# Placing the TensorE operands of a fp32r decoder step at chosen start addresses

## The chip, the cores and the metric

The kernel runs on one core of one Trainium2 chip. The metric is the device time of one execution in microseconds (us), the median of several runs. All engine times below come from one profiled execution of the kernel.

## The reference

One inference step of one decoder layer, for 256 new prompt tokens and 8 decode tokens together, with model width 2048. The large products are a first SwiGLU feed-forward (2048 to 5632 and back), an input projection to a mixer (RWKV-7 heads beside a convolution), an output projection, a memory cross-attention with its key, value, query and output projections, and a second SwiGLU:

```python
def trunk_layer(x, shift_prev, conv_prev, wkv_prev, mk, mv, p):
    x = layer_norm(ALPHA * x + 0.5 * swiglu(x, p['ffn1_w1'], p['ffn1_w3'], p['ffn1_w2']), ...)
    mix, sh, cv, wkv = parallel_mixer(x, shift_prev, conv_prev, wkv_prev, p)
    x = layer_norm(ALPHA * x + mix, ...)
    x = layer_norm(ALPHA * x + mem_attend(x, mk, mv, p['w_mq'], p['w_mo']), ...)
    x = layer_norm(ALPHA * x + 0.5 * swiglu(x, p['ffn2_w1'], p['ffn2_w3'], p['ffn2_w2']), ...)
    return x, sh, cv, wkv
```

Every weight is fp32 and is read once from HBM; the result must be close to fp32.

## The kernel before

Activations lie transposed, features on the 128 partitions and the T = 264 tokens along the free axis, so 2048 features are 16 tiles of 128 x 264. To reach fp32 accuracy with fp32r matmuls, every operand is split into a high part (rounded to fp32r) and a low part (the rest), and each product is three matmuls into the same accumulator (`mm3`, L301 to L305): high weights by high activations, high weights by low activations, low weights by high activations. In each of them the weights, 128 x 128, are the stationary operand, loaded anew for every matmul, and a 264-column activation tile is the moving operand.

Weights arrive in 512 KB chunks (128 x 1024) by SyncE's queue into `wraw` (3 buffers), ScalarE rounds each into `whi` (L188), and VectorE subtracts that from the raw chunk into `wlo` (L189); `whi` and `wlo` have 4 buffers each. The order of all the chunks is a plan written beforehand; side work (norms, RWKV heads, convolution, decode attention) is woven in as generators that step when the planned time of the main stream reaches them. `gemm` (L318) runs over the chunks; a chunk 256 columns wide uses each activation tile for two weight slices in a row, one 128 wide (the last two of each feed-forward's output, and some of the mixer's) for one.

The high and low activation tiles live in these pools:

- `act`: `xh0`, `xl0` to `xh15`, `xl15`, and the residual tiles `y0` to `y15`; in the second feed-forward the first 16 gate pairs reuse the `x` places.
- `ffn1` and `ffn2`: gate pairs `gh`, `gl`.
- `raw`: `rh`, `rl`, 266 columns each, the input of the second feed-forward, and the memory tokens in the attention stage.
- `mem`: `mh`, `ml`, 256 columns, the memory tokens during the first norm. In `mem_kv` the keys take the memory tile as moving operand; the values swap the roles, so there `whi` and `wlo` are the moving operands and the memory tiles the weights.

A tile of 264 fp32 columns takes 1,056 bytes of each partition, which is 4 x 256 + 32. Pools lie one behind another in SBUF in the order in which they are opened, and a tile's size is rounded up to 32 bytes, so the place of each tile follows from the sizes ahead of it. `place` (L82) allocates a pool's tiles in a stated order with gaps in bytes between them, which fixes their places for the rest of the pool's life. The constants' pool begins at byte 16,512 and holds 7,168 bytes, so `wraw` begins at 23,680, and `whi`, `wlo` and `act` (68,736) all at a multiple of 256 plus 128. As the buffers are 4,096 bytes and a slice of 128 columns 512, every weight slice begins at 128 modulo 256. The gap of 224 ahead of `act` puts the first `xh` at 96 modulo 256, and the tiles follow at steps of 32: `xh` and `xl` of an even tile at 96 and 128, of an odd one at 160 and 192, then a filler (four `y` tiles or 128 bytes) that brings the next even tile to 96 again. `gate_places` does the same. `rh` and `rl` begin at 96 and 160, `mh` and `ml` at 128.

Of the kernel before, what the change touches and what calls it, by code (L numbers as in the profile page):

```python
# [8 lines left out]
F32 = mybir.dt.float32  # L9
F32R = mybir.dt.float32r  # L10
# [8 lines left out]
KD = 16  # L19
TP = 256  # L20
TB = 8
T = TP + TB
DFF = 5632
# [17 lines left out]
class Side:  # L41


    def __init__(self, tc, gen, at, pace=1.0):
        self.tc, self.gen, self.next, self.done, self.pace = tc, gen, at, False, pace
# [8 lines left out]
class Builder:  # L54
    def __init__(self, tc, I, O, es):
        self.tc, self.nc, self.I, self.O = tc, tc.nc, I, O
        self.n = 0
        P = lambda name, bufs, **kw: es.enter_context(tc.tile_pool(name=name, bufs=bufs, **kw))
        self.const = P("const", 1)
        self.wraw = P("wraw", NRAW)  # L60
        self.whi = P("whi", NSPLIT)
        self.wlo = P("wlo", NSPLIT)
        self.act = P("act", 1)
        self.places()
        self.tmp = P("tmp", 2)
        self.acc = P("acc", 4, space=PSUM)
        self.mis_stack = es.enter_context(ExitStack())
        self.banks()
        self.dram = P("dram", 1, space=DRAM)
        self.t = 0.0  # L70
        self.sides = []
        self.plan, self.raws, self.split = [], [], []
        self.nraw = self.nsplit = self.nused = self.nres = 0
# [15 lines left out]
                tag, cols, dt = t  # L89
                pool.tile([128, cols], dt, tag=tag, name=self.uid(tag))  # L90

    def places(self):


        order = [224]
        for q in range(KD // 2):
            for k in (2 * q, 2 * q + 1):
                order += [(f"xh{k}", T, F32R), (f"xl{k}", T, F32R)]
            order += [(f"y{m}", T, F32) for m in range(4 * q, 4 * q + 4)] if q < KD // 4 else [128]
        self.place(self.act, *order)  # L100

    def gate_places(self, pool, first, gap):
        order = [gap]
        for i in range(first, DFF // 256, 2):
            for k in (i, i + 1):
                order += [(f"gh{k}", T, F32R), (f"gl{k}", T, F32R)]
            order.append(128)
        self.place(pool, *order)

    def uid(self, s):  # L110
        self.n += 1
        return f"{s}_{self.n}"

    def ct(self, shape, name, dt=F32):
        return self.const.tile(shape, dt, tag=name, name=name)

    def misc(self):
# [1255 lines left out]
    def att_start(self, pool):  # L1373
        nc = self.nc
        self.mx = pool
        self.banks(1)
        self.mem_reload()
        eye = self.mt("eye", (128, TB, TB), F32R)
        z = self.mt("eye0", (128, TB * TB))
        nc.vector.memset(z, 0.0)  # L1380
        nc.vector.memset(z[:, 0 : TB * TB : TB + 1], 1.0)
        nc.scalar.activation(eye.rearrange("p a b -> p (a b)"), z, AF.Copy)
        self.eye = eye
        self.kvn = {}
        self.qs = {}
        self.oh = None
# [304 lines left out]

PRETURN = 5
RAW, RENORM = 2, 0.6
GAPS = 128, 224, 96, 128
TS = 384
LASTCOLS = [(1536, 256), (1792, 128), (1920, 128)]
CONV_GAP = 2.5
# [25 lines left out]
def program(tc, I, O):  # L1723
    with ExitStack() as es:
# [10 lines left out]
        with tc.tile_pool(name="mem", bufs=1) as mpool:  # L1735
            b.place(mpool, GAPS[0])
            with tc.tile_pool(name="ffn1", bufs=1) as pool:
                b.gate_places(pool, 0, GAPS[1])
                b.xs = b.load_x(mpool)
# [31 lines left out]
        def after():  # L1771
            mix.close()
            b.raw = es.enter_context(tc.tile_pool(name="raw", bufs=1))
            for k in range(KD):
                b.place(b.raw, 128 if k else GAPS[2], (f"rh{k}", T + 2, F32R), (f"rl{k}", T + 2, F32R))
            b.att_start(att.enter_context(tc.tile_pool(name="att", bufs=1)))
# [12 lines left out]
        with tc.tile_pool(name="ffn2", bufs=1) as pool:  # L1789
            b.gate_places(pool, KD, GAPS[3])  # L1790

# [82 lines left out]
```

## Time and profile before

| | |
|---|---|
| runs | 2517.45, 2523.19, 2524.93 us; median 2523.19 |
| profiled execution | 2526.33 us |
| span of its instructions | 2524.6 us |
| granted TensorE clock, mean | 0.993 |
| TensorE matmul busy | 2470.9 us, 98% |
| VectorE / ScalarE / GpSimd busy | 1582.8 / 1195.0 / 261.7 us |
| DMA | 497.89 MB, mean 197 GB/s |

The span runs from the first to the last instruction; 1.7 us of the execution lie outside it. Matmuls are pipelined and overlap, so a matmul's own duration (0.28 us) is over twice the distance from its start to the next one's; what counts for throughput is that distance, called the pace below.

### The profile page before, as it was taken

To read this page: it belongs to the slowest core of one execution; us is meant where nothing else is said; L and a number is where in the kernel's file an instruction comes from. 1 tells how busy PE (TensorE), PEld (TensorE's weight loads), DVE (VectorE), ACT (ScalarE), POOL (GpSimd) and SP (SyncE) were. 2 spreads that over 40 slices of the span, in tenths; PEclk is the share of its full clock that TensorE was granted. 3 is DMA by queue.
4 is the path that set the end of the run, shared out by engine and by line. 5 is a ranking of instruction groups with operands and counts; after the bars stand their busy time and mean duration, and the time that the engine had idled before them with its cause. 6 is when DMAs were issued, how large, how long until landed. Compare 5 with 4: busy or idle time off the path is not lost. (4 is left out here: it accounts for less than half of the span.)

```text
span 2524.6 us, 53420 instructions
## 1 busy us (share of the span) xinstructions
PE 2470.9 (98%) x22328; PEld 2417.2 (96%) x22328; DVE 1582.8 (63%) x2545; ACT 1195.0 (47%) x1802; POOL 261.7 (10%) x422
## 2 busy tenths in 40 slices
PE   9999999999999999999989999999999999999998
PEld 9999999999999988988889888989999999999998
DVE  5545444444557599799777566789655545554465
ACT  5444433444446555455646354657444434444443
POOL 1300000000000001000110222220132500000000
PEclk9999999999999999999999999999999999999999
DMA  7656655555557754544476799976677755655554
GB/s 228 188 183 220 203 183 182 183 183 178 179 181 212 221 151 132 149 131 139 128 251 224 262 293 305 322 226 191 195 215 217 237 182 184 183 178 183 176 180 131
DMA packets 452211, 497.89 MB, mean 197 GB/s; under 512 B 22096, under 2 KB 418640, under 8 KB 451968
## 3 DMA queue, kind: packets, MB, share of 16 engines
q1 hardware_dynamic: 417840, 417.09, 54.0%
q0 software_dynamic: 20992, 67.22, 8.4%
q10 hardware_dynamic: 13136, 10.15, 1.2%
q8 instruction: 175, 2.87, 0.5%
q14 instruction: 68, 0.56, 0.1%
HBM read 477.76 MB, written 16.63 MB: 196 GB/s over the span
## 5 line engine op out<-in xcount | busy, mean ns | idle before, releaser
L189 DVE TENSOR_TENSOR wlo<-raw,whi 128x1024 fp32r<-128x1024 f32 (+1 forms) x791 | 961.4, 1216 | 850.6 <-ACT whi L188 847.3
L188 ACT ACTIVATE whi<-raw 128x1024 fp32r<-128x1024 f32 (+1 forms) x791 | 823.0, 1041 | 1035.6 <-PE acc L304 856.6
L303 PE MATMUL acc<-xh,whi 128*128 128x264 f32 x2864 | 828.7, 290 | 15.3 <-DVE y L1243 7.3
L304 PE MATMUL acc<-xl,whi 128*128 128x264 f32 x2864 | 820.2, 287 | 0.6 <-DVE xl L189 0.6
L305 PE MATMUL acc<-xh,wlo 128*128 128x264 f32 x2864 | 816.7, 286 | 0.5 <-DVE wlo L189 0.5
L303 PEld LDWEIGHTS acc<-xh,whi 128*128 128x128 f32 x2864 | 540.3, 189 | 23.8 <-ACT rh L1328 7.5
L304 PEld LDWEIGHTS acc<-xl,whi 128*128 128x128 f32 x2864 | 542.0, 189 | 3.7 <-DVE xl L189 0.8
L305 PEld LDWEIGHTS acc<-xh,wlo 128*128 128x128 f32 x2864 | 541.0, 189 | 2.3 <-DVE wlo L189 1.1
L303 PE MATMUL acc<-rh,whi 128*128 128x264 f32 (+2 forms) x1600 | 456.8, 285 | 0.2 <-ACT lnx L397 0.2
L305 PE MATMUL acc<-rh,wlo 128*128 128x264 f32 (+2 forms) x1600 | 454.5, 284 | 0.0
L304 PE MATMUL acc<-rl,whi 128*128 128x264 f32 (+2 forms) x1600 | 453.4, 283 | 0.0
L304 PE MATMUL acc<-gl,whi 128*128 128x264 f32 x1408 | 400.2, 284 | 0.0
L305 PE MATMUL acc<-gh,wlo 128*128 128x264 f32 x1408 | 400.1, 284 | 0.0
L303 PE MATMUL acc<-gh,whi 128*128 128x264 f32 x1408 | 399.5, 284 | 0.0
L303 PEld LDWEIGHTS acc<-rh,whi 128*128 128x128 f32 x1600 | 300.8, 188 | 2.2 <-ACT lnx L397 0.4
L304 PEld LDWEIGHTS acc<-rl,whi 128*128 128x128 f32 x1600 | 301.7, 189 | 1.2
L305 PEld LDWEIGHTS acc<-rh,wlo 128*128 128x128 f32 x1600 | 300.7, 188 | 0.2
L305 PEld LDWEIGHTS acc<-gh,wlo 128*128 128x128 f32 x1408 | 264.5, 188 | 0.1
L304 PEld LDWEIGHTS acc<-gl,whi 128*128 128x128 f32 x1408 | 264.5, 188 | 0.0
L303 PEld LDWEIGHTS acc<-gh,whi 128*128 128x128 f32 x1408 | 264.3, 188 | 0.1
L1176 DVE SCALAR_TENSOR_TENSOR y<-u,cw,y 128x256 f32<-128x256 f32 x240 | 111.1, 476 | 0.6
L397 ACT ACTIVATE lnx<-acc 128x264 f32<-128x264 f32 x84 | 32.4, 386 | 64.8 <-PE acc L305 64.8
(350 smaller groups left out, 2089.9 us busy)
## 6 DMA issues: line engine op xcount, KB each, us to landing
raw<-in_ffn_w SPq DMA_DIRECT2D x509, 512.0 KB, 3.6
raw<-in_w_in SPq DMA_DIRECT2D x86, 512.0 KB, 3.8
raw<-in_w_mk SPq DMA_DIRECT2D x32, 512.0 KB, 3.4
raw<-in_w_mv SPq DMA_DIRECT2D x32, 512.0 KB, 5.4
raw<-in_w_out SPq DMA_DIRECT2D x32, 512.0 KB, 5.1
kv<-in_cache_mem_k POOLq DMA_DIRECT2D x32, 512.0 KB, 6.2
raw<-in_w_mq SPq DMA_DIRECT2D x32, 512.0 KB, 5.2
kv<-in_cache_mem_v POOLq DMA_DIRECT2D x32, 512.0 KB, 6.1
```

The costliest lines, as they stand in the source:

```text
L188: a = self.nc.scalar.activation(hi, src, AF.Copy)
L189: return a, self.nc.vector.tensor_tensor(lo, src, hi.bitcast(F32), ALU.subtract)
L303: nc.tensor.matmul(out, wh, xh, start=start, stop=False)
L304: nc.tensor.matmul(out, wh, xl, start=False, stop=False)
L305: self.mark = nc.tensor.matmul(out, wl, xh, start=False, stop=stop)
L397: self.lastfn = self.nc.scalar.activation(*args, **kw)
L1176: V.scalar_tensor_tensor(c[:, :TP], u[:, i : i + TP], w(i), c[:, :TP], ALU.mult, ALU.add)
```

## The change

The order of the tiles in their pools changes, and a few small tiles change pool. Nothing that is computed changes, and no matmul, load or split is added or taken away.

- `opposite`, a new function, takes high/low pairs three at a time (a, b, c) and lays six tiles out as two sets of three neighbours: `ha`, `hb`, `la`, and `hc`, `lb`, `lc`. Sets are followed by a filler of 160 bytes modulo 256, so that each set (3 x 32 = 96) begins at the same place modulo 256. A pair left over is laid with a 32-byte gap between high and low.
- With a gap of 96 ahead of it, the first tile of `act` begins at 224, so in each set the three begin at 224, 0 and 32 modulo 256.
- The fillers in `act` are five `y` tiles (5,280 bytes, which is 160 modulo 256), two groups of small constants taken from the constants' pool (`omu`, `omka`; `nkk`, `sign`, `eps0` to `eps2`), and plain gaps.
- The constants' pool loses 320 bytes and gains a 64-byte gap tile, 256 less in all.
- The gaps ahead of `mem`, `ffn1`, `raw` and `ffn2` change from 128, 224, 96, 128 to 0, 224, 224, 128.
- In `att_start`, a temporary tile (`eye0`) is taken from the four `lnx` buffers.

```diff
+        self.const.tile([128, 16], F32, tag="gap", name="gap")
...
+    def opposite(self, pairs, fill=()):
+        sets, n = [], len(pairs) // 3 * 3
+        for t in range(0, n, 3):
+            (ha, la), (hb, lb), (hc, lc) = pairs[t : t + 3]
+            sets += [[ha, hb, la], [hc, lb, lc]]
+        sets += [[h, 32, l] for h, l in pairs[n:]]
+        fill, order = list(fill), []
+        for i, s in enumerate(sets):
+            order += s
+            if i + 1 < len(sets):
+                order += fill.pop(0) if fill else [160]
+        return order + [t for f in fill for t in f]
+
     def places(self):
-        order = [224]
-        for q in range(KD // 2):
-            for k in (2 * q, 2 * q + 1):
-                order += [(f"xh{k}", T, F32R), (f"xl{k}", T, F32R)]
-            order += [(f"y{m}", T, F32) for m in range(4 * q, 4 * q + 4)] if q < KD // 4 else [128]
-        self.place(self.act, *order)
+        x = [[(f"x{p}{k}", T, F32R) for p in "hl"] for k in range(KD)]
+        y = [(f"y{m}", T, F32) for m in range(KD)]
+        small = [("omu", 27, F32), ("omka", 8, F32)], [(n, 8, F32) for n in ("nkk", "sign", "eps0", "eps1", "eps2")]
+        fill = [y[:5], y[5:10], y[10:15], *small]
+        self.place(self.act, 96, *self.opposite(x, fill), y[15])
+        self.inact = {t[0]: t[1] for f in small for t in f}
 
     def gate_places(self, pool, first, gap):
-        order = [gap]
-        for i in range(first, DFF // 256, 2):
-            for k in (i, i + 1):
-                order += [(f"gh{k}", T, F32R), (f"gl{k}", T, F32R)]
-            order.append(128)
-        self.place(pool, *order)
+        g = [[(f"g{p}{i}", T, F32R) for p in "hl"] for i in range(first, DFF // 256)]
+        self.place(pool, gap, *self.opposite(g))
...
     def ct(self, shape, name, dt=F32):
+        if name in self.inact:
+            return self.act.tile([128, self.inact[name]], dt, tag=name, name=name)[:, : shape[1]]
         return self.const.tile(shape, dt, tag=name, name=name)
...
-        z = self.mt("eye0", (128, TB * TB))
+        z = self.t1("lnx", bufs=4)[:, : TB * TB]
...
-GAPS = 128, 224, 96, 128
+GAPS = 0, 224, 224, 128
```

## Rows read from the trace of the kernel before

**Rows 1.** The page's first part (engine, busy time and share of the span, instructions), and the granted clock in the 40 slices of its second part.

```profile
PE 2470.9 (98%) x22328; PEld 2417.2 (96%) x22328; DVE 1582.8 (63%) x2545; ACT 1195.0 (47%) x1802; POOL 261.7 (10%) x422
PEclk9999999999999999999999999999999999999999
```

**Rows 2.** Who waited for whom on all engines, the two longest totals (us in total, times, longest), and below them TensorE's own, the three longest.

```profile
ACT whi L188 <- PE acc L304: 856.6, 525, 4.0
DVE wlo L189 <- ACT whi L188: 847.3, 590, 4.4
...
PE acc L303 <- DVE y L1243: 7.3, 1, 7.3
PE acc L303 <- ACT y L1419: 6.7, 4, 5.2
PE mis L1557 <- DVE p L1446: 4.5, 3, 2.2
```

**Rows 3.** TensorE's groups of instructions by line and shape (out <- moving, weights by the program's names; columns; count, busy us and mean ns of one; idle before). Of the three lines of `mm3` the first is shown where all three have the same count.

```profile
L303 PE MATMUL acc<-xh,whi 128*128 128x264 f32 x2864 | 828.7, 290 | 15.3 <-DVE y L1243 7.3 <-ACT y L1419 5.6 <-ACT whi L188 2.0
...
L303 PE MATMUL acc<-gh,whi 128*128 128x264 f32 x1408 | 399.5, 284 | 0.0
...
L303 PE MATMUL acc<-rh,whi 128*128 128x264 f32 x1280 | 362.2, 283 | 0.2 <-ACT lnx L397 0.2
L303 PE MATMUL acc<-rh,whi 128*128 128x256 f32 x192 | 57.0, 297 | 0.0
L303 PE MATMUL acc<-whi,rh 128*128 128x256 f32 x192 | 56.0, 292 | 1.1 <-ACT y L1419 1.1
...
L303 PE MATMUL acc<-rh,whi 128*128 128x266 f32 x128 | 37.6, 294 | 0.0
L303 PE MATMUL acc<-mh,whi 128*128 128x256 f32 x64 | 18.5, 289 | 0.0
L303 PE MATMUL acc<-whi,mh 128*128 128x256 f32 x64 | 18.1, 283 | 0.0
```

**Rows 4.** Busy time and, in brackets, the number of instructions that overlap each of three stretches (us from the span's start): `x` tiles of the first feed-forward, its gate tiles, and the `r` tiles of the second. Then the granted clock, the DMA share and GB/s.

```profile
100.00:200.00 100.00, 100.00 (x826) 100.00 (x825) 49.38 (x55) 42.59 (x54) 0.00 (x0) 1.00 0.59 180
300.00:380.00 80.00, 80.00 (x662) 80.00 (x661) 36.93 (x41) 29.69 (x30) 0.00 (x0) 1.00 0.59 181
2125.00:2375.00 250.00, 250.00 (x2060) 250.00 (x2059) 124.44 (x133) 104.71 (x129) 3.88 (x8) 1.00 0.60 183
```

**Rows 5.** TensorE in order of time, 806 to 818 us: the first and the last of 102 matmuls, a value unit with the memory tiles at 128 as weights and `whi`, `wlo` at 128 as moving operand (start us, duration us).

```profile
805.82 0.28 PE L304 MATMUL acc<-wlo,mh 128*128 128x256 f32 x1
...
817.93 0.28 PE L303 MATMUL acc<-whi,mh 128*128 128x256 f32 x1
```

**Rows 6.** The same view, 1357 to 1366 us: the first and the last of 79 matmuls, a value unit with the memory tiles at 96 and 160 as weights and `whi`, `wlo` at 128 as moving operand.

```profile
1356.79 0.28 PE L304 MATMUL acc<-wlo,rh 128*128 128x256 f32 x1
...
1365.98 0.28 PE L304 MATMUL acc<-wlo,rh 128*128 128x256 f32 x1
```

**Rows 7.** The same view, 755 to 762 us: the first and the last of 60 matmuls of the first feed-forward's output, chunks 256 columns wide (each gate pair is used for two weight slices in a row).

```profile
754.77 0.28 PE L304 MATMUL acc<-gl,whi 128*128 128x264 f32 x1
...
761.93 0.28 PE L303 MATMUL acc<-gh,whi 128*128 128x264 f32 x1
```

**Rows 8.** The same view, 765.5 to 772 us: the first and the last of 55 matmuls of the same product, chunks 128 columns wide (a new gate pair for every weight slice).

```profile
765.22 0.28 PE L303 MATMUL acc<-gh,whi 128*128 128x264 f32 x1
...
771.88 0.28 PE L303 MATMUL acc<-gh,whi 128*128 128x264 f32 x1
```

**Rows 9.** The instructions that fill the identity tile of the decode attention in `att_start` (duration ns least, median, most; start us).

```profile
L1380 DVE MEMSET eye<- x1: 112/112/112, 1289.1 to 1289.1; 128x64 f32 x1
L1381 DVE MEMSET eye<- x1: 65/65/65, 1289.4 to 1289.4; 128x8 f32 x1
L1382 ACT ACTIVATE eye<-eye x1: 240/240/240, 1289.9 to 1289.9; 128x64 fp32r<-128x64 f32 x1
```

## The prediction

> **What bounds the kernel now.** I read the page's first part and the clock line first. TensorE is busy for 2470.9 of 2524.6 us and the granted clock is at its upper level, 2.4 GHz, in all 40 slices [rows 1], so neither gaps nor the throttle leave much to win. Then the waits: the two longest totals are ScalarE waiting for matmuls to free a weight buffer (856.6 us) and VectorE waiting for ScalarE behind it (847.3 us), while TensorE's longest wait for anyone is one of 7.3 us [rows 2]. The splits stand behind the matmuls and not the other way round. What sets the end is therefore the number of matmuls times their pace, start to start.
>
> The number: the three lines of `mm3` hold 2,864 + 1,408 + 1,280 + 192 + 128 = 5,872 matmuls each with the activations as moving operand and a 264-, 256- or 266-column form, together 17,616; the memory units with `mh` add 3 x 64, the swapped value units 3 x (192 + 64) [rows 3]. That is 18,576.
>
> The pace: a matmul lasts 0.28 us, so 2.3 of those that overlap a stretch began before it. Without them the three stretches give 100 / 823.7 = 121.4 ns, 80 / 659.7 = 121.3 ns and 250 / 2,057.7 = 121.5 ns [rows 4]. 18,576 x 121.4 ns is 2,255 us, 89% of the span. At 2.4 GHz, 264 columns take 110.0 ns, so 11.4 ns of each matmul is something else. The change can only work on that part. One ns per matmul is 18.6 us or 0.74% of the time; the 0.3% that a measurement of this kernel can tell from no change is 7.6 us, 0.41 ns per matmul.
>
> **The change part by part.** *Where the operands land.* The weights stay at 128: the constants' pool shrinks by 256 bytes. `act` then begins at 128 again and its gap of 96 leads to 224. A set of three spans 96 and each filler 160 modulo 256, so in each group of three pairs high and low begin at (224, 32), (0, 0), (224, 32); before it was (96, 128), (160, 192) in turn. `rh` and `rl` go from (96, 160) to (224, 32), which is the same pair moved by 128, and `mh`, `ml` from 128 to 0. Measured from the weights' 128, the moving operands stood 32 below to 64 above and will stand 96 to 160 above, on the far side of the 256 bytes.
>
> *Does the trace show that this matters?* It holds no matmul at the new places, so the price is bounded from the nearest rows. They are the value units, where the moving operand is the same (`whi`, `wlo` at 128, 256 columns) and only the weights' place differs. With weights at 128 too, 102 starts take 12.11 us, 12.11 / 101 = 119.9 ns [rows 5]; with weights at 96 and 160, 79 starts take 9.19 us, 9.19 / 78 = 117.8 ns [rows 6]. So equal places cost 2.1 ns per matmul against places 32 bytes apart. The Trainium skill says otherwise: by "SBUF — State Buffer", section "Who interferes with whom", TensorE reads the moving operand and the weights through two independent ports and waits for no one, so an address could change nothing; the trace disagrees by the 2.1 ns just read, and by the page alone this change would leave the time at that of before, a rival below.
>
> *First term, the tiles that lose distance zero.* The low tiles of even pairs stand at 128: of the (2,864 + 1,408) x 3 = 12,816 matmuls on `x` and gate tiles a third have a low tile, and half of those are even, 2,136. The memory units with `mh`, `ml` are 64 x 6 = 384 more. 2,520 x 2.1 ns = 5.3 us gained. The other end is nothing: the third stretch of rows 4 has no tile at distance zero and is no faster than the other two (121.5 against 121.4 and 121.3). I take 5.3, since rows 5 and 6 differ in nothing but the places.
>
> *Second term, all others.* 16,056 matmuls go from 32 or 64 bytes of distance to 96 or more. The low end is no gain (distance 64 is as fast as 32, rows 4 again). The high end is the same step once more, 16,056 x 2.1 ns = 33.7 us; a loss of that size is the third rival's. I choose a quarter of the high end, 8.4 us, nearer to nothing because rows 4 show no slope between 32 and 64.
>
> *Third term, the order of the places.* A chunk 256 wide uses each pair twice, 7.16 us / 59 = 121.4 ns [rows 7]; with a new pair for each slice the same tiles give 6.66 us / 54 = 123.3 ns [rows 8]. So the succession of places costs up to 1.9 ns. After the change two pairs in three have the succession that `rh`, `rl` already have (up by 64, down by 64, same again: 121.5 ns), and one in three stays at one place throughout, whose nearest row is 119.9 ns at 256 columns [rows 5], where the same-place rows are also those of distance zero. Between these I put nothing.
>
> *The rest.* The five small tiles that move are operands of the same instructions; no instruction is added, and VectorE (63%) and ScalarE (47%) have room [rows 1]. The `eye0` tile in a `lnx` buffer concerns three instructions of 112 + 65 + 240 = 417 ns around 1289 us [rows 9]. Were they to wait for the buffer, VectorE's next weight split would be late by some tenths of a us, and four weight buffers lie between that and TensorE. Nothing. No DMA is added or moved past another in any queue.
>
> Sum: 5.3 + 8.4 = 13.7 us gained. The profiled execution's 2526.3 us (1.7 us of it outside the span) would become 2512.6. It lies 3.1 us above the median of the runs, 2523.2, so the median to expect is 2509.5, about **2510 us**.
>
> **The rivals.** *It does nothing measurable:* 2516 to 2531, middle 2523. For it: three stretches with different places and successions have one pace within 0.2 ns [rows 4], and the 11.4 ns may be a cost of each fp32r matmul whatever its address. Against it: 2.1 ns between rows 5 and 6. The skill's page named above stands on this side.
>
> *Slower:* the far side is where moving reads and the weight load collide. The moving stream takes 1,056 bytes in the time in which the weights for the next matmul take 512, so the two run through the 256 bytes at different rates, and which start is best needn't be the one farthest away. The price is that of the worst succession in the trace, 123.3 - 121.4 = 1.9 ns [rows 7, 8], on all 18,576: 35 us, 2558. It decides from 0.41 ns per matmul on. For it: rows 8 show that these tiles can be slower. Against it: rows 8 concern a rare form, and the pair (96, 160) that only moves by 128 keeps its own succession.
>
> *Much faster:* half of the 11.4 ns is a clash with the weights that goes altogether, 18,576 x 5.7 = 106 us, 2417. Against it: a value unit out of the clash at 117.8 ns still stands 11.1 ns above its 106.7 ns of columns [rows 6].
>
> **How the numbers follow.** The likeliest, a gain of one to thirty-nine us by places, has 0.46 with a range of its own of 2484 to 2515; much faster 0.04; no measurable change 0.27; slower 0.23. Faster is 0.46 + 0.04 = 0.50. For 8 in 10 the range leaves out the much faster case and a little of the likeliest's end below 2486 (all 18,576 at 2.1 ns would be 2484), and above it the upper half of the slower case, from 2545 on (some 22 of the 35 us).
>
> **What would show it right or wrong.** The pace in the three stretches of rows 4: about 120.7 ns where I expect 0.7 ns gained on average. The stretch on `rh`, `rl` is the cleanest, since only the distance changes there: unmoved at 121.5 it would say that distance does nothing beyond 32 bytes, above 123 that the far side is the bad one. The value units of rows 5 should fall from 119.9 to about 117.8. Stretches on `x` and gate tiles should gain more than that on `rh`, by the first term; if they alone moved, up or down, it would be the succession and not the distance. Waits on TensorE and the clock line should stay. The prediction falls if the pace moves by more than 2.1 ns either way, or if the paces stand still and the time moves by waits.

## The result and the profile after

The changed kernel takes 2535.25 us (median of 6 runs, 2530.01 to 2541.41) against 2522.94 for the kernel before on the same chips (6 runs, 2517.45 to 2524.93). The ratio is 1.0053 with an interval of 1.0034 to 1.0073: 12 us slower, where I had forecast 13 us faster. The time lies inside the range, on its other side.

The page's first part shows the same picture as [rows 1]: TensorE busy throughout, the others with room. Its execution took 2530.01 us.

```profile
PE 2483.5 (98%) x22328; PEld 2431.6 (96%) x22328; DVE 1579.0 (62%) x2545; ACT 1195.3 (47%) x1802; POOL 260.1 (10%) x422
```

The three stretches of [rows 4], with `x`, gate and `r` tiles, and a fourth with the `r` tiles at 266 columns (stretch, then busy us and number of overlapping instructions of TensorE's matmuls, of its weight loads and of the other engines, clock, DMA):

```profile
100.00:200.00 100.00, 100.00 (x816) 100.00 (x816) 49.32 (x54) 41.51 (x54) 0.00 (x0) 1.00 0.57 179
300.00:380.00 80.00, 80.00 (x652) 80.00 (x652) 36.29 (x40) 28.93 (x30) 0.00 (x0) 1.00 0.56 177
2125.00:2375.00 250.00, 250.00 (x2054) 250.00 (x2054) 125.25 (x135) 104.28 (x129) 3.86 (x8) 1.00 0.58 182
...
1740.00:1775.00 35.00, 35.00 (x294) 35.00 (x293) 33.36 (x68) 28.13 (x49) 0.00 (x0) 1.00 0.57 177
```

Read as before, without the 2.3 that began earlier: 100 / 813.7 = 122.9 ns, 80 / 649.7 = 123.1 ns, 250 / 2,051.7 = 121.85 ns and 35 / 291.7 = 120.0 ns. Against 121.4, 121.3 and 121.5 the `x` and gate tiles lost 1.5 and 1.8 ns per matmul and the `r` tiles 0.35. The clock is at its upper level in each stretch and no matmul in the first three waited. So the loss is in the pace, as the forecast gain should have been, and most of it sits in the 12,816 matmuls on `x` and gate tiles. Over the whole trace, taking every pair of successive starts less than 0.2 us apart, their mean pace goes from 121.5 to 122.8 ns, and 12,816 x 1.3 = 17 us; the wider steps between their starts, where other work stands between, took 112.9 instead of 118.6 us. The `r` tiles lose 2.5 us more by the same count, and the 384 matmuls of 266 columns give 2 us back (below). The busy time of TensorE grew by less, by 12.6 us, from 2470.9 [rows 1] to 2483.5, which is about the 12 us of the medians. Its idle time (span less busy time) was 53.7 us before and is 44.8 here; in a second execution of the changed kernel it was 50.4. So the two profiled executions differ by only 3.7 us in time, and the rest lies within the 8 to 11 us by which executions of one kernel differ.

A value unit of the changed kernel, in order of time, the first and the last of 103 matmuls with the weights at 0 and the moving operand at 128 (start us, duration us), where before both stood at 128 [rows 5]:

```profile
812.82 0.28 PE L318 MATMUL acc<-whi,ml 128*128 128x256 f32 x1
...
824.92 0.28 PE L318 MATMUL acc<-whi,ml 128*128 128x256 f32 x1
```

12.10 us / 102 = 118.6 ns against 119.9: 1.3 of the 2.1 ns that the first term forecast here. The kernel in the old weave does not repeat it (below, at the first term).

### The profile page after: what moved, and what is told of

The parts are those of the page before. It is cut to its first block, busy times and chain, and to the rows that moved or that the text cites. A ratio compares the mean times of both kernels' runs of the same rounds, so it can differ in the third digit from the quotient of the medians.

```text
span 2528.3 us, 53419 instructions
## 1 busy us (share of the span) xinstructions
PE 2483.5 (98%) x22328; PEld 2431.6 (96%) x22328; DVE 1579.0 (62%) x2545; ACT 1195.3 (47%) x1802; POOL 260.1 (10%) x422
```

## Distance or weave: the two exchanged

The change does two things to the tiles: it moves them to the far side of the weights, and it lays them in threes instead of fours. Four runs take these apart.

**Old weave, far side.**

```diff
-        order = [224]
+        order = [96]
```

> The kernel before with one number changed: the gap ahead of act is 96 instead of 224, so every activation tile moves down by 128 bytes (x and gate pairs at 224, 0 and 32, 64; rh, rl at 224, 32; memory tiles at 0) in the old order of fours, with the weights at 128 as they were. Theory 'distance' (the far side is what costs): the loss of the changed kernel comes back, +10 to +16 us, and the pace on x and gate tiles is 122.7 to 123.1 ns. Theory 'order' (the weave in threes is what costs, near or far): the time of before within 5 us, x and gate tiles at 121.4 ns, rh tiles at about 121.9.

Measured: 2535.7 us, ratio 1.0054 (1.0041 to 1.0067). The same three stretches:

```profile
100.00:200.00 100.00, 100.00 (x816) 100.00 (x816) 49.32 (x54) 41.59 (x54) 0.00 (x0) 1.00 0.56 179
300.00:380.00 80.00, 80.00 (x653) 80.00 (x653) 36.58 (x40) 29.10 (x30) 0.00 (x0) 1.00 0.57 178
2125.00:2375.00 250.00, 250.00 (x2054) 250.00 (x2053) 124.46 (x134) 104.59 (x129) 3.86 (x8) 1.00 0.56 181
```

The counts are those of the changed kernel to one matmul, 122.9, 122.9 and 121.85 ns. The distance alone costs the whole loss.

**New weave, near side.**

```diff
-        self.place(self.act, 96, *self.opposite(x, fill), y[15])
+        self.place(self.act, 224, *self.opposite(x, fill), y[15])
```

> The changed kernel with the gap ahead of act at 224 instead of 96: every activation tile moves up by 128 bytes, so the weave in threes stands at 96, 128 and 160, beside the weights' 128. Theory 'distance': the time of the kernel before within 5 us, x and gate tiles at 121.4 ns. Theory 'order': the loss stays, +10 to +16 us, x and gate tiles at 122.7 to 123.1 ns. A mixed result (both kernels lose half) would mean that distance and order add up.

Measured: 2520.56 us, ratio 0.9989 (0.9978 to 1.0000).

```profile
100.00:200.00 100.00, 100.00 (x827) 100.00 (x826) 50.34 (x55) 41.45 (x53) 0.00 (x0) 1.00 0.57 183
300.00:380.00 80.00, 80.00 (x662) 80.00 (x662) 37.06 (x40) 29.69 (x31) 0.00 (x0) 1.00 0.59 181
2125.00:2375.00 250.00, 250.00 (x2060) 250.00 (x2059) 124.46 (x134) 106.25 (x133) 1.93 (x4) 1.00 0.56 180
```

121.25, 121.3 and 121.5 ns: the paces of [rows 4]. Everything else of the change (the weave, fillers, moved constants, the `lnx` buffer) is in this kernel and costs nothing that can be told.

**The changed kernel again.**

> The changed kernel once more, on the chip of the other runs: 1.0053 times the kernel before (interval 1.0034 to 1.0073), by every theory. Its profile shows whether the pace of 122.9 ns on x and gate tiles and 121.9 on rh tiles is the same in another execution.

Measured: 2533.73 us, ratio 1.0048 (1.0036 to 1.0060). Its stretches on `x` and `r` tiles count what they counted in the other execution:

```profile
100.00:200.00 100.00, 100.00 (x816) 100.00 (x816) 48.43 (x53) 41.97 (x54) 0.00 (x0) 1.00 0.57 178
...
2125.00:2375.00 250.00, 250.00 (x2054) 250.00 (x2053) 125.39 (x134) 104.74 (x129) 3.86 (x8) 1.00 0.57 182
```

**All moved together.** Is it the distance from the weights, or the absolute place?

```diff
         self.const = P("const", 1)
+        self.const.tile([128, 32], F32, tag="gap", name="gap")
```

> The kernel before with a 128-byte gap tile at the front of the constants' pool: weights, activations and all else move up by 128 bytes together. Weights begin at 0, x and gate pairs at 224, 0 and 32, 64: the absolute places of the far kernel, the distances of the kernel before. If only the distance between moving operand and weights counts (theory 'distance') or only the order of the places (theory 'order'), the time of before within 3 us and 121.4 ns. If the absolute place of the moving operand counts, +10 to +16 us, as in the far kernel.

Measured: 2518.42 us, ratio 0.9984 (0.9976 to 0.9993).

```profile
100.00:200.00 100.00, 100.00 (x827) 100.00 (x826) 49.59 (x55) 42.38 (x54) 0.00 (x0) 1.00 0.58 182
300.00:380.00 80.00, 80.00 (x661) 80.00 (x660) 36.93 (x41) 29.69 (x30) 0.00 (x0) 1.00 0.58 181
2125.00:2375.00 250.00, 250.00 (x2060) 250.00 (x2060) 124.03 (x132) 105.39 (x131) 2.36 (x5) 1.00 0.57 181
```

121.25, 121.45 and 121.5 ns. The activation tiles begin at the same places modulo 256 as in the far kernel with the old weave; what differs is where the weights, the raw chunks and the constants begin. Of these the main stream of matmuls reads only the weights. So the place of the moving operand relative to the weights decides, and not the place by itself. The moving tiles of the two kernels lie 256 bytes apart, but the groups of tiles step by 256 as well, so that `x` and gate tiles pass through the multiples of 256 in either kernel. That it is the weight load which collides with the moving stream is the natural reading, and not shown; no run separates it from the engines that write the weight tiles. The 4 us by which this kernel lies below the one before are a little more than the 3 us allowed for, and are not explained.

## The distances between

Four runs of the kernel before with only the gap ahead of `act` changed, to 288, 160, 256 and 192.

> The kernel before with all activation tiles 64 bytes further up (weights stay at 128): x and gate pairs stand 32, 64 and 96, 128 bytes above the weights' place, rh, rl 32 and 96 above, the memory tiles 64 above. Theory 'the nearer the better' (pace rises with the distance, 121.4 ns within 64 bytes and 122.8 at 96 to 192): half the tiles far, about 122.1 ns and +5 to +8 us. Rival 'only the band below and at the weights is fast': as the far kernel, +11 to +15 us. Rival 'only distances beyond 128 cost': no change within 3 us.

Measured: 2532.88 us, 1.0035 (1.0018 to 1.0052).

```profile
100.00:200.00 100.00, 100.00 (x821) 100.00 (x820) 49.67 (x55) 41.43 (x53) 0.00 (x0) 1.00 0.59 180
...
2125.00:2375.00 250.00, 250.00 (x2048) 250.00 (x2047) 125.46 (x134) 104.08 (x129) 3.88 (x8) 1.00 0.59 182
```

> The kernel before with all activation tiles 64 bytes further down: x and gate pairs stand 96 and 64 below and 32 below and level with the weights, rh, rl 96 and 32 below, the memory tiles 64 below. Theory 'the nearer the better': half the tiles far, about 122.1 ns and +5 to +8 us, the same as 64 up. Rival 'one side of the weights is the good one': one of the two shifts by 64 loses 11 us or more and the other nothing or gains.

Measured: 2528.78 us, 1.0021 (1.0005 to 1.0037).

```profile
100.00:200.00 100.00, 100.00 (x824) 100.00 (x823) 49.94 (x55) 41.88 (x54) 0.00 (x0) 1.00 0.59 182
...
2125.00:2375.00 250.00, 250.00 (x2038) 250.00 (x2038) 123.56 (x131) 103.29 (x128) 3.88 (x8) 1.00 0.59 180
```

> The kernel before with all activation tiles 32 bytes further up: distances 0, 32 and 64, 96. 'The nearer the better': a quarter of the tiles far, 0 to +4 us. With 'one side is good': of the sign of the run 64 up and about half its size.

Measured: 2519.97 us, 0.9980 (0.9965 to 0.9994).

```profile
100.00:200.00 100.00, 100.00 (x828) 100.00 (x827) 49.34 (x54) 42.94 (x55) 0.00 (x0) 1.00 0.59 180
...
2125.00:2375.00 250.00, 250.00 (x2063) 250.00 (x2062) 125.46 (x135) 104.30 (x130) 3.88 (x8) 1.00 0.59 182
```

> The kernel before with all activation tiles 32 bytes further down: 64 and 32 below, level and 32 above. 'The nearer the better': all tiles within 64, so 121.4 ns and within 4 us of before; it might be a little faster, as the middle of the band is then on the weights. With 'one side is good': of the sign of the run 64 down and about half its size.

Measured: 2531.32 us, 1.0028 (1.0014 to 1.0043).

```profile
100.00:200.00 100.00, 100.00 (x824) 100.00 (x823) 49.33 (x54) 42.41 (x55) 0.00 (x0) 1.00 0.59 180
...
2125.00:2375.00 250.00, 250.00 (x2048) 250.00 (x2047) 124.94 (x134) 104.53 (x129) 3.87 (x8) 1.00 0.59 181
```

| shift of the tiles | `x` pairs, distance from the weights | `x` pace | `r` pace | ratio |
|---|---|---|---|---|
| -64 | -96 to 0 | 121.7 | 122.8 | 1.0021 |
| -32 | -64 to 32 | 121.7 | 122.2 | 1.0028 |
| 0 (before) | -32 to 64 | 121.4 | 121.5 | 1 |
| +32 | 0 to 96 | 121.1 | 121.3 | 0.9980 |
| +64 | 32 to 128 | 122.1 | 122.2 | 1.0035 |
| +128 (far, old weave) | 96 to 192 | 122.9 | 121.85 | 1.0054 |

The far kernel moved its tiles 128 bytes down, which is the same as 128 up modulo 256. The paces come from one stretch of one execution each. The curve on `x` tiles has its low point around 0 to 96 and rises on both sides; the time follows it roughly. "The nearer the better" misses that -32, with all tiles within 64, is no better than -64, and that +32, with a quarter of the tiles at 96, is the best. The two sides are not alike. Among these six shifts 1.8 ns from end to end are what `x` tiles win or lose, and the kernel before stood 0.3 ns from the lowest. The `r` tiles stand at other distances in the same kernels (-96 and -32 at -64, up to 96 and 160 at +128) and have a curve of their own. At -32 and +64 one stretch is not the whole story: there the gate tiles ran slower by 1.1 ns in some other stretches (next section).

**The threes at the low point**, the changed kernel with a gap of 256 ahead of `act`:

> The changed kernel with the gap ahead of act at 256: the weave in threes at 128, 160 and 192, that is level with the weights and 32 and 64 above. If the places count and not the weave, as the two runs with exchanged weave and distance said: a little faster than before, as the old weave 32 up (0.998), 121.0 to 121.3 ns on x and gate tiles, -3 to -7 us. If threes and fours differ after all, outside of that.

Measured: 2519.41 us, 0.9991 (0.9979 to 1.0003).

```profile
100.00:200.00 100.00, 100.00 (x826) 100.00 (x825) 49.50 (x55) 42.55 (x54) 0.00 (x0) 1.00 0.58 181
300.00:380.00 80.00, 80.00 (x659) 80.00 (x659) 36.75 (x41) 29.71 (x30) 0.00 (x0) 1.00 0.57 181
```

121.4 and 121.8 ns: no gain in the pace, unlike the fours 32 up (121.1 on both), so the weave matters by 0.3 to 0.7 ns here. The time doesn't tell it from before.

## Columns, and a pace that depends on what went before

In the changed kernel the 266-column matmuls ran at 120.0 ns. Two runs take the 266 columns to all the `r` matmuls of the second feed-forward (`norm, n, self.renormed = None, T + 2, True` for `None, T, True`), once with the tiles where they were, once with `GAPS` at 128, 224, 224, 0, which moves the `r` tiles alone to 224 and 32.

> The kernel before, except that all matmuls on the r tiles of the second feed-forward take 266 columns (3,840 of them took 264; the two more columns are not used), tiles where they were, 96 and 160. Theory 'two streams' (what costs is how the moving stream and the weight load of the next matmul fall on each other, so the number of columns must count as well as the distance): all of them run at the 125.4 ns that the 384 matmuls of 266 columns have before, 3,840 x 4.2 ns = +16 us. Rival 'the distance alone': two columns more are 0.8 ns, +3 us.

Measured: 2535.22 us, 1.0054 (1.0041 to 1.0067).

```profile
2125.00:2375.00 250.00, 250.00 (x2006) 250.00 (x2005) 122.93 (x133) 102.37 (x127) 3.88 (x8) 1.00 0.57 178
```

250 / 2,003.7 = 124.8 ns. Two columns more cost 3.3 ns, where the rival expected 0.8; the time, 13 us longer, lies near the +16 of the first theory.

> The same with the r tiles at 224 and 32, as in the changed kernel, all other tiles where they were before. Theory 'two streams': all of them at the 120.3 ns that the 384 matmuls of 266 columns have in the changed kernel, 3,840 x 0.9 ns + 384 x 5.1 ns = 5.4 us less than before: for 266 columns the far side would be the good one. Rival 'the far side is bad': 121.9 + 0.8 = 122.7 ns, +5 us.

Measured: 2524.86 us, 1.0011 (0.9999 to 1.0023): neither theory. The stage in three stretches:

```profile
1745.00:1890.00 145.00, 145.00 (x1211) 145.00 (x1210) 91.92 (x128) 75.18 (x114) 31.68 (x37) 1.00 0.67 207
1905.00:1990.00 85.00, 84.76 (x679) 84.33 (x678) 40.41 (x40) 33.68 (x44) 31.69 (x38) 1.00 0.75 219
2125.00:2375.00 250.00, 250.00 (x2085) 250.00 (x2085) 126.34 (x135) 107.97 (x134) 3.36 (x7) 1.00 0.58 184
```

120.0 ns, then 84.76 / 676.7 = 125.3, then 120.0 again, with the same tiles, columns and weight places. The middle stretch holds two short breaks; start to start between them the pace is 124.5. Between the first two stretches TensorE waited once for an accumulator (start us, duration us; in brackets the idle time before it and what ended it):

```profile
1895.31 0.39 PE L303 MATMUL acc<-rh,whi 128*128 128x266 f32 x1 [0.88 <-ACT lnx L397]
```

Up to that wait the starts are 120.0 ns apart, from some matmuls after it 124.5.

The kernel before, looked at again in that stage (266 columns, then two stretches of 264):

```profile
1740.00:1775.00 35.00, 35.00 (x279) 34.94 (x279) 33.42 (x69) 27.53 (x47) 0.00 (x0) 1.00 0.58 176
...
1800.00:1890.00 90.00, 90.00 (x743) 89.98 (x741) 46.93 (x47) 38.01 (x51) 28.21 (x31) 1.00 0.73 214
1905.00:1985.00 80.00, 80.00 (x669) 80.00 (x668) 43.17 (x43) 33.98 (x43) 28.82 (x33) 1.00 0.77 225
```

35 / 276.7 = 126.5 ns for 266 columns in a stretch that holds a short break (125.4 over all 384, start to start); then 90 / 740.7 = 121.5 and 80 / 666.7 = 120.0 ns for 264, and between the last two one wait for the same releaser, 1880 to 1910 us:

```profile
PE acc L303 <- ACT lnx L397: 0.2, 1, 0.2
```

So on the `r` tiles the stream holds one of at least two paces for hundreds of matmuls, and the pace changes at a short wait, to the better or the worse.

The gate tiles do the same in two of the layouts. The first feed-forward uses the same 22 gate pairs in both of its halves. In the kernel shifted by -32 they ran at 80 / 657.7 = 121.6 ns in the first and at 60 / 488.7 = 122.8 in most of the second:

```profile
300.00:380.00 80.00, 80.00 (x660) 80.00 (x659) 36.74 (x40) 29.63 (x30) 0.00 (x0) 1.00 0.60 181
700.00:760.00 60.00, 60.00 (x491) 60.00 (x490) 33.39 (x47) 24.95 (x31) 0.00 (x0) 1.00 0.60 181
...
670.85 0.70 PE L349 MATMUL mis<-lns,ones 128*128 128x264 f32 x2
```

The pace changes at the last row, where two matmuls of the layer norm stand between the second and the third matmul of a product, without a wait. In the kernel shifted by +64 the gate pairs of the second feed-forward ran at 90 / 729.7 = 123.3 ns in the first half and at the start of the second, until the same two matmuls in the same position brought them to 70 / 572.7 = 122.2:

```profile
2020.00:2110.00 90.00, 90.00 (x732) 90.00 (x731) 41.28 (x46) 32.99 (x34) 1.99 (x4) 1.00 0.58 184
2410.00:2480.00 70.00, 70.00 (x575) 70.00 (x575) 41.87 (x65) 32.47 (x45) 0.00 (x0) 1.00 0.57 180
...
2406.31 0.64 PE L349 MATMUL mis<-lns,ones 128*128 128x264 f32 x2
```

That a break of the stream, a wait or side matmuls, stands at these changes of pace is shown. Not every break changes it: in the changed kernel the `r` stream was held up at 1828.7 us, waited for 0.6 us at 1875.8 and ran at 121.9 ns before and after either. The load of DMA does not explain the slow pace either: it goes with a DMA share of 0.75 and 219 GB/s in the run above, while the kernel before ran at 120.0 ns under 0.77 and 225 GB/s. That the break is the cause, by setting the two streams anew against each other, is argued.

This does not touch the comparison of near and far. In the kernel before and in the four others with `x` and gate tiles in the same band (the near kernel, all moved together, the two with 266 columns) the means over 20 us of the `x` and gate matmuls lie between 121.2 and 121.5 ns in both feed-forwards, and in the three executions on the far side between 122.6 and 123.1. (The first 20 us are left out, and the end from 2470 us on, where the chunks are 128 columns wide.)

**Parts put together**: the old weave 32 up, and the `r` tiles far with 266 columns.

> Parts put together: the old weave 32 up (x and gate pairs 128, 160 and 192, 224), the r tiles at 224 and 32, all their matmuls with 266 columns in the second feed-forward. By the paces read so far: x and gate tiles 121.15 instead of 121.5 ns, 12,816 x 0.35 = 4.5 us, and 5.4 us from the r tiles: -10 us, 0.996. If the r part fails, -3 us at best.

Measured: 2527.56 us, 1.0017 (1.0002 to 1.0031), with runs from 2515.81 to 2534.86.

```profile
2125.00:2375.00 250.00, 250.00 (x2011) 250.00 (x2011) 123.47 (x133) 102.72 (x128) 3.87 (x8) 1.00 0.57 179
```

250 / 2,008.7 = 124.5 ns: the `r` tiles lie at the same bytes as in the far run with 266 columns above, whose pace here was 120.0. This execution held the slow pace. 4,224 matmuls of 266 columns x 4.5 ns = 19 us, as much as the whole spread of this kernel's runs; that the other executions differ by this is possible, but only one was profiled. None of the twelve is a version to prefer by more than 0.2%.

## Why the prediction was wrong

**What bounds it** was right: the pace of the 18,576 matmuls carries the effect, and waits do not.

**The first term** (5.3 us from leaving distance zero) was not found. The value units that ran at 118.6 ns in the changed kernel ran at 12.24 us / 102 = 120.0 ns in the far kernel, whose operands begin at the same places modulo 256, if not at the same bytes (in order of time, the first and the last of 103 matmuls):

```profile
812.76 0.28 PE L305 MATMUL acc<-whi,ml 128*128 128x256 f32 x1
...
825.00 0.28 PE L305 MATMUL acc<-whi,ml 128*128 128x256 f32 x1
```

The near kernel with the weave in threes has more low and high tiles at distance zero than the kernel before, and the same pace. Nor was the difference between [rows 5] and [rows 6] one of places alone, as I took it: start to start, the units of [rows 6] ran at 117.9 ns with the memory tiles at 224 and 32 as well (the far kernel), and at 120.0 with them at 32 and 96 (shifted by -64), away from the weights. So 2.1 ns was not the price of equal places.

**The second term** is the step that failed. I bounded what happens beyond 64 bytes by a gain of 2.1 ns and a loss of the size of the rival "slower", and chose a quarter of the gain because [rows 4] show no slope between 32 and 64. No slope there said nothing of 96 to 192: the runs show 122.9 instead of 121.4 ns on `x` and gate tiles, a loss of 1.5 ns where I took a gain of 0.5. The nearest rows all lay close to the low point of a curve, within the band in use, and I drew a gain on beyond it. The 2.1 ns that the gain was a quarter of also came from the first term, where it was misread.

**The third term** (order of places, taken as nothing) was right for the two places tried: the exchanged runs put the weave at 0 to 0.1% of the time, though 32 bytes up threes and fours differ by some tenths of a ns.

**The rivals.** "Slower" had the right direction and place, a far side that costs; that the two streams collide there is its explanation, and not shown. Its price of 1.9 ns on all matmuls was too wide, as the `r` and memory matmuls lost little or nothing. I gave it 0.23. The rule of the Trainium skill ("SBUF — State Buffer", "Who interferes with whom"), two independent ports and no waiting, would have left the time as it was; the far kernel and the one with all moved together, 122.9 against 121.25 ns with the moving tiles at the same places modulo 256, disagree with it.

**What I named as telling signs:** the stretch on `rh`, `rl` was to be the cleanest. It moved by 0.35 ns only and would have read as "distance does nothing". One reason it misled is that its pace also depends on the state that the stream is in, 120.0 or 121.5 ns in the kernel before alone. The `x` and gate stretches, which hold one pace throughout in the kernel before and in the changed one, were the ones to read. "If they alone moved it would be the succession" was wrong: the exchange shows the distance.

**The edits costed at nothing** (constants, `lnx` buffer, fillers) cost nothing, by the near kernel.

## What to carry to other kernels

Where a stream is limited by its own pace, the start addresses of the two operands relative to each other can matter: here 0.7% of the time lay between the best and the worst (0.9980 to 1.0054). They are found by shifting one gap and counting starts in clean stretches, on both sides, since a trend within the band that is in use does not carry beyond it. Move one thing at a time: distance, order and column count each changed the pace, and a layout change mixes all three. A single stretch can hold a faster or slower pace that depends on what broke the stream before it, so compare several stretches and executions.

## What was unexpected of the hardware

At 256 columns the pace with both operands level is 119.9 ns, and with the memory tiles 64 below the weights (the kernel shifted by -64; the first and the last of 108 matmuls, which pass from keys to values, start us and duration us) it is 12.12 us / 107 = 113.3 ns, in both roles:

```profile
790.78 0.28 PE L304 MATMUL acc<-ml,whi 128*128 128x256 f32 x1
...
802.90 0.28 PE L303 MATMUL acc<-whi,mh 128*128 128x256 f32 x1
```

With the memory tiles 64 above it is 117.8 ns (the kernel shifted by +64, first and last of 96):

```profile
790.74 0.28 PE L305 MATMUL acc<-mh,wlo 128*128 128x256 f32 x1
...
801.93 0.28 PE L304 MATMUL acc<-ml,whi 128*128 128x256 f32 x1
```

113.3 ns and 120.0 ns are 272 and 288 cycles of 2.4 GHz. In the keys the moving operand is 64 below the weights and in the values 64 above, at the same pace, so the distance with its sign is not the whole rule either; what else enters stays open. And the pace has states: 120.0 or 124.5 ns for the same 266 columns of the `r` tiles at the same bytes, and 121.6 or 122.8 for the same gate tiles.
